# A Fourier group folded over tokens t and 256-t, in a one-layer encoder block on one core

## The chip, the cores and the metric

The kernel runs on one core of one Trainium2 chip. The metric is the device time of one execution in microseconds. The kernel before takes 934.45 us (median of three runs, 934.38 to 934.88). TensorE is the matrix engine (PE in the profile), VectorE is DVE, ScalarE is ACT, GpSimd is POOL, and SyncE (SP) issues most of the DMAs. Every engine takes its instructions in the order in which the program lists them; an instruction that waits holds up all that stand behind it on the same engine.

## The reference

One layer with 256 tokens of width 2048: a norm, a combined projection, attention heads beside Fourier groups, an output projection, a second norm, a gated feed-forward part with a short convolution, and a last norm.

```
h = RMSNorm(x)
[q | k | v | u] = h @ w_in          # 12 query heads, 4 key and value heads, u has 512 columns
a = RMSNorm(window_attention(q, k, v))
# Fourier group: u as 4 groups g of 128 channels c, s = the token
f = real(fft2(u[s, g, c], axes=(s, c), norm='ortho'))
y = einsum('sgc,gcd->sgd', f, w_fourier)
x = x + concat[a, RMSNorm(y)] @ w_out
x = x + conv_ffn(RMSNorm(x)) ; out = RMSNorm(x)
```

The real part of the two-dimensional transform is, in the positions, a product of u with cos and one with sin, for the frequencies 0 to 128 and 1 to 127; the rest follow by symmetry. In the channels it is folded with w_fourier into one small matrix each for the cosine part and the sine part.

## The kernel before, in words

Precision comes from splitting: a float32 matrix is written as a high part (rounded to TensorE's fast type) and a low part (the rest), and a product is made of three products: high by high, high by low, low by high. ScalarE writes a high part, VectorE subtracts and writes the low part.

The weights come in *units* of 1 MB (128 partitions by 2048). Units 0 to 3 are the columns of u (they come together with the transposed tokens), 4 to 7 those of v, 8 to 23 the sixteen key and query heads (k0, q0, q1, q2, k1, ...), 24 to 39 the output projection; then the feed-forward part follows. The function `unit(i, work)` sets the order by hand: it runs what is listed *before* unit i, then the unit's matmuls, then what is listed *beside* it, then `step(i)`, which splits unit i+2 (`split_high` on ScalarE, `split_low` on VectorE, after which SP issues the load of a later unit into one of three buffers), then what is listed *behind* it. The lists are filled with `at(beside, i, f, ...)`.

A unit of v (`moving_weights`, lines 347 to 349) is 24 matmuls of 512 columns. A unit of a head (`still_weights`, line 364) takes for each of 16 blocks one matmul with the high part of the weights against 512 columns and one with the low part against 256; it begins with two high ones, so it needs the low part almost at once.

The part around the change:
- The norm's row sums come from ScalarE (`token_sums`); `token_scales` makes the scale of each token, r1, with a power on GpSimd, beside unit 4. A token's scale is one value per partition. As a row (r1b, the same 256 values on each partition) it is needed to scale the keys; `row_by_hbm` (lines 318 to 322, behind unit 4) writes it value by value to HBM from GpSimd's queue and reads it back on all partitions.
- Beside unit 5, `rows_out` (466, 467) scales u from the two PSUM banks ps_u[0] (tokens 0 to 127) and ps_u[1] (tokens 128 to 255) and writes u_hi and u_lo. `fourier_positions` (530, 531) splits the table of cos and sin of the positions, 256 columns for each token block.
- Before unit 6, `fourier_weights` (545) makes the channel matrices; `fourier_weights_out` (552) copies them from PSUM as G.
- Before unit 7, `fourier_rows` (566) makes the position transform: four groups, two token blocks, three products each, 24 matmuls of 256 columns into one bank a group (ps_f). Beside unit 7 the four results go to SBUF (575, 577).
- Before units 8 to 11, `fourier_channels` (585) makes one group each (ps_y): two plain float32 matmuls, of 129 and 127 columns. Beside it the copy (593), behind it the join of the two halves (598 to 602), beside the next unit the output (`feature_out`: square, high part, low part, 495, 296, 297).
- The heads run beside units 9 and later: query head h in unit s has its scores before unit s+2, softmax beside it, and its values some units later.

Of the kernel before, what the change touches and what calls it, by code (L numbers as in the profile page):

```python
# [21 lines left out]
NG = 4  # L22
# [8 lines left out]

U_HEAD, U_ROW = 16, 768


SHIFT = 16

# [82 lines left out]
def block_kernel(  # L119
# [19 lines left out]
    nc = tc.nc  # L139
# [75 lines left out]
    cat_pool = pa.enter_context(tc.tile_pool(name="cat", bufs=16))  # L215
# [2 lines left out]
    vec = base.tile([P, 232], F32, tag="vec", name="vec")  # L218
    chan = cat_pool.tile([P, 512], F32, tag="cat", name="chan")[:, 0 : 2 * P]
    wfs = cat_pool.tile([P, FW], F32, tag="cat", name="wfs")  # L220
    pos = cat_pool.tile([P, 2, S], F32, tag="cat", name="pos")
    Gs = [cat_pool.tile([P, FW], F32, tag="cat", name=f"G{c}") for c in range(2)]
    pos_hi = cat_pool.tile([P, 2, S], F32R, tag="cat", name="pos_hi")
    pos_lo = cat_pool.tile([P, 2, S], F32R, tag="cat", name="pos_lo")
# [62 lines left out]
    ps = bank(dn, "ps_warm")  # L287
# [27 lines left out]

    rows = ctx.enter_context(tc.tile_pool(name="rows", bufs=1, space=bass.MemoryType.DRAM))

    def row_by_hbm(r, dst, name):

        row = rows.tile([2, P], F32, tag="row" + name, name="row" + name)  # L320
        nc.gpsimd.dma_start(row.rearrange("b p -> p b"), r)
        nc.gpsimd.dma_start(dst, row.rearrange("b p -> (b p)").partition_broadcast(P))


    def blocks_out(src, t, name):
# [73 lines left out]
    for c in range(4):  # L399
        t = base.tile([P, 4, 512], F32R, tag=f"hT{c}", name=f"hT{c}")  # L400
        hT.append(t)
    ps_u = [bank(mm, f"ps_u{b}") for b in range(2)]
    for k in range(NK):
        c, q = k // 4, k % 4
        if q == 0:
            hi, lo = (t.rearrange("p (k c) -> p k c", k=4) for t in parts_of(c))
        n = 1 if c < 2 else 2
# [3 lines left out]
        if q % n == 0:  # L411
            w, h = u_part(k, 0, FW, n), hi[:, q : q + n, :]
# [3 lines left out]
        if k < 4:  # L416

            for p, w in enumerate([hi, hi, lo]):
                for b in range(2):
                    o = p % 2 * S + b * P  # L420
                    nc.tensor.matmul(
                        ps_u[b], hk(k)[:, o : o + P], w[:, q, :],
                        start=k == 0 and p == 0, stop=False,
# [9 lines left out]
    ph = pa.enter_context(tc.tile_pool(name="pa", bufs=1))  # L433
# [4 lines left out]
    r1 = base.tile([P, 2], F32, tag="rstd1", name="rstd1")  # L438
# [23 lines left out]
    def rows_out(hi, lo, ps):  # L462

        for b in range(2):
            r = r1[:, b : b + 1]
            nc.scalar.activation(hi[:, b, :], ps[b], AF.Copy, scale=r)
            nc.vector.scalar_tensor_tensor(
                lo[:, b, :], ps[b], r, f32(hi[:, b, :]), ALU.mult, ALU.subtract
            )
# [7 lines left out]
    u_hi, u_lo = row_parts("u")  # L477
    v_hi, v_lo = row_parts("v")
    r1b = ph.tile([P, S], F32, tag="r1b", name="r1b")
    for c in range(2, 4):  # L480
        at(beside, 4, token_sums, c)
    at(beside, 4, lambda: fourier_parts())
    at(beside, 4, token_scales)
    at(beside, 5, rows_out, u_hi, u_lo, ps_u)
    at(behind, 5, query_scales)

    cat = {}

# [38 lines left out]
    held = {}  # L527

    def fourier_positions():
        nc.scalar.activation(pos_hi, pos, AF.Copy)  # L530
        nc.vector.tensor_tensor(pos_lo, pos, f32(pos_hi), ALU.subtract)

    def fourier_parts():
        for src, (hi, lo) in (
# [18 lines left out]

    H = S // 2
    us = []

    def fourier_rows():
        for g in range(NG):  # L560
            ps = held["f", g] = bank(dn, f"ps_f{g}")
            for b in range(2):
                for n, (u, w) in enumerate(
                    [(u_hi, pos_hi), (u_hi, pos_lo), (u_lo, pos_hi)]
                ):
                    nc.tensor.matmul(
                        ps[:, 0:S], u[:, b, g * P : (g + 1) * P], w[:, b, :],
                        start=b == 0 and n == 0, stop=b == 1 and n == 2,
                    )

    def fourier_rows_out():
        for g in range(NG):
            t = ph.tile([P, 512], F32, tag="sc", name=f"uf{g}", bufs=4)[:, 0:S]
            if g % 2:
                nc.scalar.activation(t, held.pop(("f", g))[:, 0:S], AF.Copy)
            else:
                nc.vector.tensor_copy(t, held.pop(("f", g))[:, 0:S])
            us.append(t)

    sq_f = ph.tile([P, S], F32, tag="sqf", name="sq_f")  # L580

    def fourier_channels(g):
        ps = held["y", g] = bank(dn, f"ps_y{g}")
        for part, o, n in ((0, 0, H + 1), (1, H + 1, H - 1)):
            nc.tensor.matmul(
# [3 lines left out]


    def fourier_channels_copy(g):
        h = held["h", g] = ph.tile([P, S], F32, tag="tmp", name=f"yh{g}", bufs=2)
        nc.scalar.activation(h, held.pop(("y", g))[:, 0:S], AF.Copy)

    def fourier_channels_join(g):
        h = held.pop(("h", g))
        y = held["y", g] = ph.tile([P, S], F32, tag="add", name=f"y{g}", bufs=2)
        nc.vector.tensor_tensor(y[:, 1:H], h[:, 1:H], h[:, H + 1 : S], ALU.add)
        nc.vector.tensor_tensor(
            y[:, H + 1 : S], h[:, H - 1 : 0 : -1], h[:, S - 1 : H : -1], ALU.subtract  # L600
        )
        nc.vector.tensor_copy(y[:, 0 : H + 1 : H], h[:, 0 : H + 1 : H])

# [13 lines left out]
    at(beside, 5, fourier_positions)  # L617
    at(before, 6, fourier_weights)
    at(beside, 6, fourier_weights_out)
    at(behind, 4, row_by_hbm, r1, r1b, "1")  # L620
    at(before, 7, fourier_rows)
    at(beside, 7, fourier_rows_out)
    at(beside, 8, lambda: rows_out(v_hi, v_lo, ps_v))
    at(behind, 8, distances)

    def fourier_channels_steps():
        for g in range(NG):
            i = 8 + g
# [255 lines left out]
    for n, (c, kq) in enumerate(OUT_ORDER):  # L884
        i = N_OUT + n
# [35 lines left out]
    r2b = fp.tile([P, S], F32, tag="r2b", name="r2b", bufs=1)  # L921
# [195 lines left out]
    held = {(c, p): bank(dn, f"ps_{p}_{c}") for c in range(2) for p in ("P1", "N5")}  # L1117
# [108 lines left out]
    def last_out_post(c, part, ps):  # L1226

        i = n_front + 2
        out_add(c, part, ps)
        flip_x_out(c)  # L1230
        for o, n in ((0, 512), (512, 1536)):
            split_low(i - 1, o, n)
        out_sums(c)
        split_high(i)
        split_low(i, 0, 1024)
        tot2 = base.tile([P, 2], F32, tag="tot2", name="tot2")
        nc.vector.tensor_reduce(tot2, ssq2, mybir.AxisListType.X, ALU.add)
        rstd_of(tot2, D, "2", r=r2b[:, 0:2])
        split_low(i, 1024, 1024, reload=False)
        nc.vector.transpose(r2b[:, 32:64], r2b[:, 0:32])  # L1240
        row = rows.tile([2, 4, 32], F32, tag="row2", name="row2")
        for b in range(2):
            nc.sync.dma_start(row[b], r2b[b:P:32, 32:64])
        flip_x_in(c)
        nc.sync.dma_start(r2b, row.rearrange("b q j -> (b q j)").partition_broadcast(P))
        load(i + RAW)

    OPEN = 4
# [2 lines left out]
    for q in range(OPEN):  # L1251
        kind, j = items[q]
        ps = bank(mm, f"ps_{kind}{j}")
# [4 lines left out]
        if q == 1:  # L1258
            i = up_index[3]
# [23 lines left out]
    for n, it in enumerate(items):  # L1283
# [8 lines left out]
        if it[0] in ("gate", "val"):  # L1292
            kind, j = it
            ps = bank(mm, f"ps_{kind}{j}")
# [4 lines left out]
        if it[0] == "product":  # L1299
            kind, g, c, p = it  # L1300
# [30 lines left out]
    i = up_index[n]  # L1331
# [54 lines left out]
def _layout(inp):  # L1386
# [3 lines left out]
    f = lambda a: np.ascontiguousarray(np.asarray(a), dtype=np.float32)  # L1390
    x = f(inp["x"]).reshape(2, P, D)
# [20 lines left out]
    start = {"q": 0, "k": AW}  # L1412
# [14 lines left out]
    def rows_by(tiles, cols):  # L1427
# [17 lines left out]
    )  # L1445
    t = np.arange(S)
    ang = 2.0 * np.pi * ((t[:, None] * t[None, :]) % S) / S
    c_pos = np.concatenate(
        [np.cos(ang[:, : S // 2 + 1]), np.sin(ang[:, 1 : S // 2])], axis=1
    )  # L1450
    c_pos = c_pos.reshape(2, P, S).transpose(1, 0, 2)
# [38 lines left out]
```

## Time and profile before

| | before |
|---|---|
| median of three runs | 934.45 us |
| the profiled execution's own time | 934.68 us |
| its span (first to last instruction) | 932.9 us |
| TensorE busy | 924.0 us, 99% |
| VectorE busy | 772.4 us, 83% |
| ScalarE busy | 542.3 us, 58% |
| granted TensorE clock | 0.997 |
| units 4 to 8 on TensorE | 27.3 to 59.4 us |

Busy time of a matmul is modelled and overlaps that of the next one, so the price of a matmul is read from the distance between starts, or from a piece of the chain that ended last. A row of a timeline gives start, duration, engine, line, operation, the tile written and those read, the count, and in brackets how long the engine stood idle before it and what released it. In the table of stretches a row gives the busy time of each engine, then the granted clock, the DMA engines' share and their GB/s. The table of DMA issues gives the time from issue to landing. On an engine that isn't the bound, idle time costs nothing.

### The profile page before, as it was taken

The numbers are of one execution on the slowest core, as the hardware profiler recorded it, in microseconds if no ns is written. First come the engines' busy times: TensorE is split into PE (matmuls) and PEld (weight loads), VectorE is DVE, ScalarE is ACT, GpSimd is POOL, SyncE is SP. The second block draws the span as 40 slices with busy tenths as digits, with TensorE's granted clock in tenths as the row PEclk, the third lists the DMA queues.
The fourth block names the chain that finished last, engine by engine and source line by source line (L and its number), as shares of the span: only waits on it lengthen the run. The fifth ranks groups of instructions, "written<-read, shape, count | busy, mean of one in ns | idle before, by whom it ended". The sixth has DMA issues, their size and how long they took to land.

```text
span 932.9 us, 12860 instructions
## 1 busy us (share of the span) xinstructions
PE 924.0 (99%) x4981; PEld 800.8 (86%) x4981; DVE 772.4 (83%) x988; ACT 542.3 (58%) x675; POOL 63.0 (7%) x80
## 2 busy tenths in 40 slices
PE   9999999999999999999999999999999999999996
PEld 7888998888888888888888888888888888888885
DVE  7668988787768877898878997888979789989995
ACT  7756776546455655566555665555755556655553
POOL 0101111200000000000000000000000000000002
PEclk9999999999999999999999999999999999999998
DMA  9965877657778668788798779887787968779652
GB/s 365 316 216 169 248 237 209 209 180 276 229 264 275 201 200 261 242 276 261 230 288 256 239 212 299 224 261 234 264 243 241 309 221 271 238 234 272 204 180 91
DMA packets 59309, 224.96 MB, mean 241 GB/s; under 512 B 24400, under 2 KB 29904, under 8 KB 35696
## 3 DMA queue, kind: packets, MB, share of 16 engines
q1 hardware_dynamic: 54560, 194.39, 58.3%
q0 software_dynamic: 4544, 29.49, 17.1%
q8 instruction: 39, 0.64, 0.3%
q10 hardware_dynamic: 144, 0.26, 0.1%
q14 instruction: 22, 0.18, 0.1%
HBM read 217.04 MB, written 7.08 MB: 240 GB/s over the span
## 4 chain that ended last, share of the span: by engine, by line
PE 98%; DMA 0%; ACT 0%; DVE 0%; issue 0%; POOLq 0%; POOL 0%; ACTq 0%
PE ps_val L364 25%; PE ps_gate L364 25%; PE ps_q L364 7%; PE ps_P L1161 3%; PE ps_P L1160 3%; PE ps_P L1162 3%; PE ps_N L1160 3%; PE ps_N L1161 3%; PE ps_N L1162 3%; PE ps_a L347 2%; PE ps_k L364 2%; PE ps_a L349 2%; PE ps_a L348 2%; PE ps_s L676 1%; PE ps_o L770 1%; PE ps_ff L347 1%
## 5 line engine op out<-in xcount | busy, mean ns | idle before, releaser
L203 DVE TENSOR_TENSOR lo<-raw,hi 128x2048 fp32r<-128x2048 f32 (+2 forms) x133 | 294.9, 2220 | 31.9 <-ACT hi L195 31.5
L195 ACT ACTIVATE hi<-raw 128x2048 fp32r<-128x2048 f32 (+1 forms) x131 | 246.8, 1886 | 28.2 <-PE ps_a L348 10.2
L364 PE MATMUL ps_gate<-hU,hi 128*128 128x512 f32 x688 | 236.2, 389 | 0.0
L364 PE MATMUL ps_val<-hU,hi 128*128 128x512 f32 x688 | 236.2, 389 | 0.0
L364 PE MATMUL ps_gate<-hU,lo 128*128 128x256 f32 x688 | 190.0, 276 | 0.0
L364 PE MATMUL ps_val<-hU,lo 128*128 128x256 f32 x687 | 189.7, 276 | 0.0
L364 PEld LDWEIGHTS ps_val<-hU,hi 128*128 128x128 f32 x688 | 129.2, 188 | 26.9
L364 PEld LDWEIGHTS ps_gate<-hU,hi 128*128 128x128 f32 x688 | 129.1, 188 | 26.8
L364 PEld LDWEIGHTS ps_gate<-hU,lo 128*128 128x128 f32 x688 | 129.2, 188 | 1.3
L364 PEld LDWEIGHTS ps_val<-hU,lo 128*128 128x128 f32 x687 | 129.0, 188 | 1.3
L941 ACT ACTIVATE ft_g<-ps_gate 128x256 f32<-128x256 f32 x43 | 16.5, 384 | 120.6 <-PE ps_gate L364 120.6
L941 ACT ACTIVATE ft_v<-ps_val 128x256 f32<-128x256 f32 x43 | 16.4, 383 | 86.7 <-PE ps_val L364 86.7
L364 PE MATMUL ps_q<-hT,hi 128*128 128x512 f32 x192 | 65.0, 391 | 0.0
L1160 PE MATMUL ps_P<-hi_P,op_P 128*128 128x512 f32 x144 | 56.1, 389 | 0.0
L1161 PE MATMUL ps_P<-hi_P,op_P 128*128 128x512 f32 x144 | 56.0, 389 | 0.0
L1162 PE MATMUL ps_P<-lo_P,op_P 128*128 128x512 f32 x144 | 56.0, 389 | 0.0
L364 PE MATMUL ps_q<-hT,lo 128*128 128x256 f32 x192 | 51.3, 277 | 0.0
L1058 DVE TENSOR_TENSOR lo_N<-sumw,hi_N 128x2048 fp32r<-128x2048 f32 (+1 forms) x20 | 41.5, 2076 | 9.4 <-ACT hi_N L1057 9.2
L1160 PE MATMUL ps_N<-hi_N,op_N 128*128 128x512 f32 x108 | 42.0, 389 | 0.0
L1161 PE MATMUL ps_N<-hi_N,op_N 128*128 128x512 f32 x108 | 42.0, 389 | 0.0
L1162 PE MATMUL ps_N<-lo_N,op_N 128*128 128x512 f32 x108 | 42.0, 389 | 0.0
L364 PEld LDWEIGHTS ps_q<-hT,hi 128*128 128x128 f32 x192 | 35.2, 188 | 6.6
(402 smaller groups left out, 1588.8 us busy)
## 6 DMA issues: line engine op xcount, KB each, us to landing
raw<-in_w_up SPq DMA_DIRECT2D x86, 1024.0 KB, 6.8
raw<-in_w_in SPq DMA_DIRECT2D x20, 1024.0 KB, 7.2
raw<-in_w_out SPq DMA_DIRECT2D x16, 1024.0 KB, 5.0
sumw<-in_w_down POOLq DMA_DIRECT2D x16, 1024.0 KB, 8.6
raw<-in_w_down_late SPq DMA_DIRECT2D x4, 1024.0 KB, 6.9
raw<-in_w_down_last SPq DMA_DIRECT2D x4, 768.0 KB, 4.3
turnp<-flip SPq DMA_DIRECT2D x44, 64.0 KB, 1.9
flop<-turnp SPq DMA_DIRECT2D x11, 256.0 KB, 3.2
```

Source lines behind the costliest of these rows:

```text
L195: nc.scalar.activation(halves[i][0][:, s], raws[i][:, s], AF.Copy)
L203: nc.vector.tensor_tensor(lo[:, s], raws[i][:, s], f32(hi[:, s]), ALU.subtract)
L347: nc.tensor.matmul(ps, ah, wh, start=first and q == q0, stop=False)
L348: nc.tensor.matmul(ps, al, wh, start=False, stop=False)
L349: nc.tensor.matmul(ps, ah, wl, start=False, stop=last and q == q0 + len(kk) - 1)
L364: nc.tensor.matmul(ps[:, x], (hi, lo)[i][:, k * P : (k + 1) * P], hk(k)[:, x], start=n == 0 and k == 0, stop=n == len(order) - 1 and k == ...
L676: nc.tensor.matmul(ps[:, b * S : (b + 1) * S], qT[:, qo + b * P : qo + (b + 1) * P], kT[:, ko : ko + S], start=n == 0, stop=n == 2,)
L941: nc.scalar.activation(tmp, ps[:, S : 2 * S], AF.Copy)
L1058: nc.vector.tensor_tensor(lo, src, f32(hi), ALU.subtract)
L1160: nc.tensor.matmul(ps, o[:, 0, p, :], hi[:, s], start=first and p == 0, stop=False)
L1161: nc.tensor.matmul(ps, o[:, 1, p, :], hi[:, s], start=False, stop=False)
L1162: nc.tensor.matmul(ps, o[:, 0, p, :], lo[:, s], start=False, stop=last and p == n - 1)
```

## The change

The position transform uses the symmetry of the input as well: cos takes the same value for tokens t and 256-t, sin the opposite one. So the sum u[t] + u[256-t] needs cos alone, over 128 values of t, and the difference needs sin alone.

- Token 256-t lies on another partition of another block than t. `fold_turned` (beside unit 5) scales and copies ps_u[1] to SBUF on ScalarE, and VectorE turns it twice by 32 x 32 blocks, reversing each block of 32 tokens. `fold_back` (behind unit 5) moves the four blocks of 32 partitions to their places with five DMAs on ScalarE's queue: three of 32 partitions, one of 31, one of a single partition (2 KB a partition), into the tile `back`.
- `fold` (beside unit 6, ahead of the copies of G) adds and subtracts on VectorE, u_hi is written on ScalarE; `fold_low` (behind unit 6) writes u_lo.
- The position table has 384 columns in place of 2 x 256. Frequencies are sorted, even ones first; low parts of the tables are written into columns of their own, so that a high part of u passes over high and low columns in one matmul. `fourier_rows(g)` now has four matmuls a group, of 256, 130, 320 and 192 columns, and `fourier_rows_out(g)` adds the low columns to the high ones (ScalarE copies, VectorE adds).
- The position transform moves from before unit 7 to before unit 9, its results beside units 9 and 10, the channel steps from units 8 to 11 to units 10 to 13. The copy of a channel result becomes two copies, one with its columns put back in order.
- The norm's row goes by blocks, as the second norm's did: VectorE turns it by 32 x 32 blocks, SP writes two pieces to HBM behind unit 4 and reads the row back behind unit 5. GpSimd's two DMAs are gone.

```diff
-    def row_by_hbm(r, dst, name):
-        row = rows.tile([2, P], F32, tag="row" + name, name="row" + name)
-        nc.gpsimd.dma_start(row.rearrange("b p -> p b"), r)
-        nc.gpsimd.dma_start(dst, row.rearrange("b p -> (b p)").partition_broadcast(P))
+    def row_out(t, name):
+        nc.vector.transpose(t[:, 32:64], t[:, 0:32])
+        row = rows.tile([2, 4, 32], F32, tag="row" + name, name="row" + name)
+        for b in range(2):
+            nc.sync.dma_start(row[b], t[b:P:32, 32:64])
+        return row
+    def row_in(row, t):
+        nc.sync.dma_start(t, row.rearrange("b q j -> (b q j)").partition_broadcast(P))
...
+    def fold_turned():
+        t, w = (ph.tile([P, 512], F32, tag="sc", name=f"u_{n}", bufs=4) for n in ("1", "turned"))
+        nc.scalar.activation(t, ps_u[1], AF.Copy, scale=r1[:, 1:2])
+        nc.vector.transpose(w, t)
+        w = w.rearrange("p (f i) -> p f i", i=32)[:, :, ::-1]
+        nc.vector.transpose(t.rearrange("p (f i) -> p f i", i=32), w)
+        folded["turned"] = t
+    def fold_back():
+        t = folded.pop("turned")
+        back = folded["back"] = ph.tile([P, 512], F32, tag="sc", name="u_back", bufs=4)
+        for q in range(3, -1, -1):
+            n, p = 32 - (q == 0), 97 - 32 * q
+            nc.scalar.dma_start(back[p : p + n], t[32 * q : 32 * q + n])
+        nc.scalar.dma_start(back[0:1], t[31:32])
+    def fold():
+        back = folded.pop("back")
+        for q, op in enumerate((ALU.add, ALU.subtract)):
+            t = ph.tile([P, 512], F32, tag="sc", name=f"u_fold{q}", bufs=4)
+            nc.vector.scalar_tensor_tensor(t, ps_u[0], r1[:, 0:1], back, ALU.mult, op)
+            nc.scalar.activation(u_hi[:, q, :], t, AF.Copy)
+            folded[q] = t
+    def fold_low():
+        for q in range(2):
+            nc.vector.tensor_tensor(u_lo[:, q, :], folded.pop(q), f32(u_hi[:, q, :]), ALU.subtract)
...
+    nc.gpsimd.memset(r1b[:, 0:32], 1.0)
+    def token_row_out():
+        nc.vector.tensor_copy(r1b[:, 0:2], r1)
+        held["row"] = row_out(r1b, "1")
+    def token_row_in():
+        row_in(held.pop("row"), r1b)
...
-    at(beside, 5, rows_out, u_hi, u_lo, ps_u)
+    at(beside, 5, fold_turned)
+    at(behind, 4, token_row_out)
+    at(behind, 5, token_row_in)
     at(behind, 5, query_scales)
+    at(behind, 5, fold_back)
+    at(beside, 6, fold)
+    at(behind, 6, fold_low)
...
     def fourier_positions():
-        nc.scalar.activation(pos_hi, pos, AF.Copy)
-        nc.vector.tensor_tensor(pos_lo, pos, f32(pos_hi), ALU.subtract)
+        odd = H // 2
+        n = odd + H
+        tt = nc.vector.tensor_tensor
+        cos, last, od, sin = pos[:, 0:H], pos[:, H : H + 1], pos[:, 2 * H - odd : 2 * H], pos[:, 2 * H :]
+        nc.scalar.activation(pos_s[:, H:], cos, AF.Copy)
+        nc.scalar.activation(pos_s[:, H - 1 : H], last, AF.Copy)
+        tt(pos_s[:, 0 : H - 1], cos[:, 1:], f32(pos_s[:, H + 1 :]), ALU.subtract)
+        nc.scalar.activation(pos_d[:, 0:n], pos[:, 2 * H - odd :], AF.Copy)
+        nc.scalar.activation(pos_d[:, n + H - 1 :], sin[:, 0:1], AF.Copy)
+        tt(pos_d[:, n : n + H - 1], sin[:, 1:], f32(pos_d[:, odd + 1 : n]), ALU.subtract)
...
+    def fourier_rows(g):
+        ps = held["f", g] = bank(dn, f"ps_f{g}")
+        c, o = slice(g * P, (g + 1) * P), 2 * H - H // 2
+        for n, (t, q, x, w, s) in enumerate([
+            (u_hi, 0, pos_s, 2 * H, 0),
+            (u_lo, 0, pos_s[:, H - 2 :], H + 2, H - 2),
+            (u_hi, 1, pos_d, H // 2 + 2 * H, o),
+            (u_lo, 1, pos_d, H // 2 + H, o),
+        ]):
+            nc.tensor.matmul(
+                ps[:, s : s + w], t[:, q, c], x[:, 0:w], start=n == 0, stop=n == 3,
+                skip_group_check=True,
+            )
+    def fourier_rows_out(g):
+        ps = held.pop(("f", g))
+        low = ph.tile([P, S], F32, tag="tmp", name=f"uf_low{g}", bufs=2)
+        t = us[g] = ph.tile([P, 512], F32, tag="sc", name=f"uf{g}", bufs=4)
+        nc.scalar.activation(
+            low.rearrange("p (a k) -> p a k", a=2),
+            ps.rearrange("p (a k) -> p a k", a=4)[:, 0:4:3, :], AF.Copy,
+        )
+        nc.scalar.activation(t[:, 0:1], ps[:, H : H + 1], AF.Copy)
+        nc.vector.tensor_tensor(t[:, 1:S], ps[:, H + 1 : 3 * H], low[:, 0 : S - 1], ALU.add)
...
-        h = held["h", g] = ph.tile([P, S], F32, tag="tmp", name=f"yh{g}", bufs=2)
-        nc.scalar.activation(h, held.pop(("y", g))[:, 0:S], AF.Copy)
+        h, ps = ph.tile([P, S], F32, tag="tmp", name=f"yh{g}", bufs=2), held.pop(("y", g))
+        held["h", g] = h
+        nc.scalar.activation(
+            h[:, 0:H].rearrange("p (m e) -> p e m", e=2),
+            ps[:, 0:H].rearrange("p (e m) -> p e m", e=2), AF.Copy,
+        )
+        nc.scalar.activation(h[:, H:S], ps[:, H:S], AF.Copy)
...
-    at(behind, 4, row_by_hbm, r1, r1b, "1")
-    at(before, 7, fourier_rows)
-    at(beside, 7, fourier_rows_out)
     at(beside, 8, lambda: rows_out(v_hi, v_lo, ps_v))
+    for g in range(NG):
+        at(before, 9, fourier_rows, g)
+        at(beside, 9 + g // 2, fourier_rows_out, g)
...
-            i = 8 + g
+            i = 10 + g
             at(before, i, fourier_channels, g)
```

More of the change, by code (lines that the diff above doesn't have):

```diff
@@ L32 @@
 U_HEAD, U_ROW = 16, 768
+H = S // 2
+N_POS = 3 * H
 SHIFT = 16
@@ L220, in block_kernel @@
     wfs = cat_pool.tile([P, FW], F32, tag="cat", name="wfs")
-    pos = cat_pool.tile([P, 2, S], F32, tag="cat", name="pos")
+    pos = cat_pool.tile([P, 512], F32, tag="cat", name="pos")[:, 0:N_POS]
     Gs = [cat_pool.tile([P, FW], F32, tag="cat", name=f"G{c}") for c in range(2)]
-    pos_hi = cat_pool.tile([P, 2, S], F32R, tag="cat", name="pos_hi")
-    pos_lo = cat_pool.tile([P, 2, S], F32R, tag="cat", name="pos_lo")
+    pos_s = cat_pool.tile([P, 512], F32R, tag="cat", name="pos_s")[:, 0 : 2 * H]
+    pos_d = cat_pool.tile([P, 512], F32R, tag="cat", name="pos_d")[:, 0 : H // 2 + 2 * H]
     chan_parts = cat_pool.tile([P, 2, 2 * P], F32R, tag="cat", name="chan_parts")
@@ L477, in block_kernel @@
     u_hi, u_lo = row_parts("u")
+    folded = {}
+    def fold_turned():
[22 more added lines that the diff above has]
+            nc.vector.tensor_tensor(u_lo[:, q, :], folded.pop(q), f32(u_hi[:, q, :]), ALU.subtract)
     v_hi, v_lo = row_parts("v")
     r1b = ph.tile([P, S], F32, tag="r1b", name="r1b")
+    nc.gpsimd.memset(r1b[:, 0:32], 1.0)
[4 more added lines that the diff above has]
+        row_in(held.pop("row"), r1b)
     for c in range(2, 4):
@@ L552, in fourier_weights_out @@
             nc.scalar.activation(Gs[part], held.pop(("g", part)), AF.Copy)
[L556 to L578, printed above, removed]
+    us = {}
+    def fourier_rows(g):
[21 more added lines that the diff above has]
+        nc.vector.tensor_tensor(t[:, 1:S], ps[:, H + 1 : 3 * H], low[:, 0 : S - 1], ALU.add)
     sq_f = ph.tile([P, S], F32, tag="sqf", name="sq_f")
@@ L1239, in last_out_post @@
         split_low(i, 1024, 1024, reload=False)
[L1240 to L1243, printed above, removed]
+        row = row_out(r2b, "2")
         flip_x_in(c)
-        nc.sync.dma_start(r2b, row.rearrange("b q j -> (b q j)").partition_broadcast(P))
+        row_in(row, r2b)
         load(i + RAW)
@@ L1447, in _layout @@
     ang = 2.0 * np.pi * ((t[:, None] * t[None, :]) % S) / S
[L1448 to L1451, printed above, removed]
+    near, k = ang[:H], np.r_[np.arange(0, H, 2), np.arange(1, H, 2), H]
+    even = (k % 2 == 0) * 1.0
+    c_pos = np.zeros((P, N_POS))
+    c_pos[:, 0 : H + 1] = np.cos(near[:, k])
+    c_pos[0, 0 : H + 1] = even
+    c_pos[0, 2 * H - H // 2 : 2 * H] = 1.0
+    c_pos[1:, 2 * H + 1 :] = np.sin(near[1:, 1:H])
     k = np.arange(P)
```

## The prediction

> **What bounds the kernel now.** I read the page first (engine shares, the chain that ended last), then TensorE's waits, then the timelines of TensorE, ScalarE and VectorE from 36 us on, where the changed code runs, then the DMA views.
>
> ```profile
> PE 924.0 (99%) x4981; PEld 800.8 (86%) x4981; DVE 772.4 (83%) x988; ACT 542.3 (58%) x675; POOL 63.0 (7%) x80
> PE 98%; DMA 0%; ACT 0%; DVE 0%; issue 0%; POOLq 0%; POOL 0%; ACTq 0%
> PE ps_warm L289 <- POOL ones L281: 1.0, 1, 1.0
> PE ps_u L421 <- ACT hT L296: 0.2, 1, 0.2
> ```
>
> TensorE is the bound: its two waits lie at the very start. So a matmul taken out is worth its whole issue time, and a wait that TensorE has not had so far is lost time that nothing later gives back.
>
> **The matmuls of the position transform.** Durations of matmuls overlap, so I go by distances between starts and by pieces of the chain.
>
> ```profile
> 45.21 2.88 PE ps_f L566 x24
> 53.52 0.44 PE ps_y L585 x4
> 175.01 0.44 PE ps_t L725 x4
> 45.05 0.28 PE L566 MATMUL ps_f<-pos_hi,u_hi 128*128 128x256 f32 x1
> 47.92 0.39 PE L347 MATMUL ps_v<-hi,hT 128*128 128x512 f32 x1
> 51.78 0.39 PE L349 MATMUL ps_v<-lo,hT 128*128 128x512 f32 x1
> ```
>
> The 24 removed matmuls of 256 columns cost 2.88 us, 0.12 each; one of 512 columns costs 0.227 (17 of them lie between the last two starts, 3.86 us). So a column beyond 256 costs 0.42 ns. Each group now has four: 256 columns 0.12, 320 columns 0.12 + 64 x 0.42 ns = 0.147, and two narrower ones, 130 and 192 columns, of a kind that this kernel never runs under 256. Lower end: by the column, 0.067 and 0.093, 0.427 a group, 1.71 in all, a gain of 1.17. Upper end: the channel matmuls (ps_y) of 127 and 129 columns show two records of 0.11 each, so 0.22 for some 128 plain float32 columns; at that price 0.22 and 0.33, 0.817 a group, 3.27 in all, a loss of 0.39. [...] I take 0.11 and 0.115: 0.492 a group, 1.97 in all, **a gain of 0.91 us**. The channel matmuls are the same, two units later; the weight products (ps_g) stay.
>
> **The fold, and what queues behind it.** This is the expensive part.
>
> ```profile
> 38.36 1.27 ACT L466 ACTIVATE u_hi<-ps_u,rstd 128x512 fp32r<-128x512 f32 x2 [3.26 <-POOL rstd L307]
> 39.51 0.63 ACT L530 ACTIVATE pos_hi<-pos 128x512 fp32r<-128x512 f32 x1
> 40.03 1.91 ACT L195 ACTIVATE hi<-raw 128x2048 fp32r<-128x2048 f32 x1
> 41.84 1.07 ACT L552 ACTIVATE G<-ps_g 128x512 f32<-128x512 f32 x2
> 42.79 1.93 ACT L195 ACTIVATE hi<-raw 128x2048 fp32r<-128x2048 f32 x1
> 39.75 0.74 DVE L467 SCALAR_TENSOR_TENSOR u_lo<-ps_u,rstd,u_hi 128x512 fp32r<-128x512 f32 x1
> 41.98 2.29 DVE L203 TENSOR_TENSOR lo<-raw,hi 128x2048 fp32r<-128x2048 f32 x1 [0.90 <-ACT hi L195]
> 44.46 0.17 DVE L460 RECIPROCAL rq_inv<-rq_pos 128x2 f32<-128x2 f32 x1
> 44.75 2.29 DVE L203 TENSOR_TENSOR lo<-raw,hi 128x2048 fp32r<-128x2048 f32 x1
> 81.89 0.71 DVE L328 STREAM_TRANSPOSE flip<-sc 128x512 f32<-128x512 f32 x1
> 928.32 0.37 ACTq L1223 DMA_DIRECT2D out_y<-z_P  x1
> ```
>
> Before, ScalarE and VectorE made u's parts at 38.36 to 40.5 without waiting for any transfer, then unit 7's parts (lo done 44.27) and unit 8's (lo done 47.04). Now:
> - ScalarE copies ps_u[1] at 38.36, 0.64 (half of 1.27), done 39.0. VectorE turns it twice, 0.71 each, the second waiting for the first: 39.05 to 40.5. The copy and small transpose for the norm's row lie before that, in VectorE's idle time up to 39.08.
> - ScalarE's position copies are narrower (four, some 0.7 in all) and replace 0.63 + 0.63; unit 7's high part starts near 39.6 and ends 41.5, its low part 43.8, with the scales 44.3 as before.
> - ScalarE's queue issues five DMAs, 0.37 each. They need the second transpose (40.5) and come in program order behind unit 7's high part. If the queue runs ahead of the running activation, they go at 40.55, 40.9, 41.3, 41.66 (the 31 rows) and 42.0; if it doesn't, 0.95 later. I take the first.
> - Landing:
>
> ```profile
> turnp<-flip SPq DMA_DIRECT2D x44, 64.0 KB, 1.9
> DMA to landing us min/median/max: 1.7/2.0/5.4
> q1 hardware_dynamic: 54560, 194.39, 58.3%
> q10 hardware_dynamic: 144, 0.26, 0.1%
> 41.00:42.00 1.00, 1.00 (x6) 0.82 (x5) 0.10 (x2) 1.00 (x2) 0.00 (x0) 1.00 0.96 402
> 43.00:44.00 1.00, 1.00 (x6) 0.84 (x5) 1.00 (x1) 1.00 (x1) 0.00 (x0) 1.00 0.00 0
> ```
>
> The second row is that of the tile turnp (44 DMAs). A 32-row piece of 64 KB is like it: 1.9. The 31 rows, 62 KB, have no row like them. ScalarE's only DMA before (q10) is 128 rows in 144 packets, which is 16 engines with eight rows and one closing packet each: equal shares. 31 is prime and has equal shares on one engine only. Lower end: spread all the same, 1.9. Upper end: one engine, at the rate of 194.39 MB / (0.583 x 16 x 932.9 us) = 22.3 GB/s, 2.8 us on top: 4.7; with the slowest turnp, 8.2. The shares of q10 are the nearest row, so I take 4.7, and 0.6 for the weight loads on the same engines (share 0.96 until 42, and unit 10's load again from about 44): **landing 5.3, at 47.0**. [...] No trace here shows an uneven DMA yet.
> - Behind that wait stand, on VectorE, the two fold instructions and unit 8's low part; on ScalarE, the two high parts of u, the two G copies and unit 8's high part. From the landing: fold 0.67 + 0.75, the second u_hi 0.63, G 1.07, hi 1.92, lo 2.29, less some 0.15 for overlaps: 7.2. Unit 8's low part is done at 54.2, where it was done at 47.04.
> - TensorE gets there sooner: without ps_f in front of it unit 7 starts at 45.05, takes 24 x 0.227 = 5.45 and ends at 50.5. Unit 8 starts with two high tiles (0.45) and then needs the low part: at 50.95. Before, that need came at 54.4 against 47.04, 7 us of slack; now TensorE waits 54.2 - 50.95 = **3.25 us**. Ends: landing hidden up to 44.4 (VectorE is busy till then) gives 0.65; landing at 50 gives 6.3.
>
> **Moved and cheap parts.** The norm's row: SP issues two small DMAs behind unit 9's load and the broadcast behind unit 10's (the two loads below); SP has nothing else between them, and r1b's first reader comes at 60.34. Nothing is late by it. POOL loses two issues, and its queue has nothing else there. The change takes away the old row's writes:
>
> ```profile
> 37.78 0.33 SPq L179 DMA_DIRECT2D raw<-in_w_in  x1
> 44.30 0.33 SPq L179 DMA_DIRECT2D raw<-in_w_in  x1
> 60.34 0.42 DVE L657 TENSOR_TENSOR add_k<-add_k,r1b 128x256 f32<-128x256 f32 x1
> row<-rstd POOLq DMA_DIRECT2D x1, 1.0 KB, 11.1
> 50.30 0.59 POOL L322 DMA_DIRECT2D r1b<-row  x1 [10.73 <-DMA row<-rstd]
> ```
>
> Beside them the DMA engines moved nothing at 43 to 44 us although loads were in flight. TensorE waited for none of these loads, so I count this at nothing. The low parts of u (two of 0.69) now stand before unit 9's low part: 56.7 or so against a need near 61.
>
> The join, output and copies of the four channel groups come two units later, when attention heads run. The tightest place is the fourth head's scores:
>
> ```profile
> 95.73 0.72 PE ps_s L676 x6
> 93.36 0.42 DVE L297 SCALAR_TENSOR_TENSOR qT<-add_q,qT 128x256 fp32r<-128x256 f32 x1 [0.48 <-ACT qT L296]
> 79.17 0.28 DVE L599 TENSOR_TENSOR y<-yh 128x127 f32<-128x127 f32 x1
> 83.49 0.48 DVE L297 SCALAR_TENSOR_TENSOR cat<-y,vec,cat 128x256 fp32r<-128x256 f32 x1
> ```
>
> Its qT was ready 1.95 us ahead. VectorE gets a join (0.28 + 0.2 and the small copy, starts 0.2 apart: 0.47) in unit 12 and join and output (0.87) in unit 13, 1.34 more; TensorE gets 0.88 more there (two ps_y). VectorE also comes some 0.5 later out of unit 8 and the four row outputs. About 1 us is left, so nothing, but this cover is thin.
>
> **Sum**, against the profiled execution (934.68 us, span 932.9): -0.91 + 3.25 = +2.3, 937.0. The median of the runs shown is 0.23 lower, so **936.8**.
>
> **Rivals.**
> 1. *Hidden transfer (not slower).* The 31 rows spread over 16 engines after all and land by 44.4, beneath unit 7's low part. For: turnp's 1.9. Against: the equal shares of q10. The wait is then 0.65 and the sum -0.3: 934.2. It decides from a landing before 44.7 (wait 0.91, no change); from 46.5 on it is slower by 0.2%, about what a measurement of this kernel tells from no change (1.87 us).
> 2. *Narrow matmuls at the plain float32 price.* For: ps_y's two records. Against: no record of the split type is that slow. 1.3 more: 938.1.
> 3. *A second wait at the fourth head's scores.* ScalarE's extra copies or VectorE's row outputs use up the last 1 us and 1 more: 937.8.
> 4. *TensorE loses speed in the wait.* The trace shows a slow start although the granted clock is 1.00:
>
> ```profile
> 1.00 3.36 PE L289 MATMUL ps_warm<-ones 128*128 128x128 f32 x14 [1.00 <-POOL ones L281]
> ```
>
> That is 0.24 a record against 0.11 later. If a wait near 4 us brings this back for some 3.4 us, half of that is lost on top: with 4.3 of wait, 934.45 - 0.91 + 4.3 + 1.7 = 939.5. Against it: my wait is shorter than that. [...]
>
> **How the numbers follow.** Forecast 0.42, rival 1 0.24, rival 2 0.20, rival 3 0.08, rival 4 0.06. The forecast itself spreads with the landing (46 to 48.2), 935.8 to 938.0, and some two thirds of it lie beyond 0.2%. Slower: 0.28 + 0.19 + 0.08 + 0.06 and a little of rival 1, 0.62. Faster needs the by-column price and rival 1's landing and still more, 0.04. The same: 0.34. The range goes from rival 1 (934.2) to short of rival 4 (939.2).
>
> **What would show it.** After: one wait of TensorE in unit 8 (ps_k), released by VectorE's lo, about 3 us; ps_f in 16 records, about 1.97 us; a landing of `back` over 4 us, the 31-row piece slowest; VectorE's fold waiting for that DMA; no hole in the DMA rate at 43 to 50 us. I am wrong if `back` lands before 45, if lo for unit 8 isn't behind the fold, or if TensorE waits elsewhere.

## The result and the profile after

The changed kernel takes 942.8 us (runs of 942.67 and 942.85) against 934.39 before (median of six): ratio 1.0089, 95% interval 1.0069 to 1.0109. It is slower, by more than the range of the prediction allowed (934.2 to 939.2). Some executions, four of the six of the changed kernel among them, take 15 to 20 us longer; the times and ratios here leave them out. The traces compared are those of executions of 934.68 and 942.85 us, 8.17 apart.

The page of the changed kernel first: engine shares, the granted clock in 40 slices, and the shares of the chain that ended last.

```profile
PE 926.2 (98%) x4973; PEld 800.9 (85%) x4973; DVE 776.2 (82%) x997; ACT 544.0 (58%) x689; POOL 62.6 (7%) x79
...
PEclk9979999999999999999999999999999999999998
...
PE 93%; DMA 4%; ACT 1%; DVE 1%; SPq 0%; POOL 0%; issue 0%; ACTq 0%; POOLq 0%
```

TensorE has eight matmuls fewer and yet is busy 2.2 us longer. The chain, 98% TensorE before, now has 4% DMA and some ScalarE and VectorE. And the third slice (47 to 71 us) has a granted clock of 0.7 to 0.8. The waits of TensorE say where:

```profile
PE ps_k L372 <- ACT hi L197: 4.9, 1, 4.9
PE ps_k L372 <- DVE lo L205: 1.1, 1, 1.1
PE ps_warm L291 <- POOL ones L283: 1.0, 1, 1.0
PE ps_u L429 <- ACT hT L298: 0.2, 1, 0.2
```

The two lower rows are those of before. The two upper ones are new and both lie in unit 8 (ps_k): first its high part is missing, then its low part. The chain that ended last, in order of time (start, duration, what), leads back to the fold's transfer:

```profile
42.47 1.13 ACTq L503
...
43.64 6.31 DMA u_back<-u
...
49.97 0.07 DVE u_fold L511
...
50.64 0.75 DVE u_fold L511
...
51.95 1.06 ACT G L615 x2
53.02 1.81 ACT hi L197
...
54.85 2.30 DVE lo L205
...
57.19 7.61 PE ps_k L372 x30
64.80 1.93 PE ps_f L631 x16
```

Read it downward: the last piece lands at 49.97, then come fold, the copies of G, unit 8's high part, its low part (done 57.14), and only then do 30 of unit 8's 32 matmuls run, in 7.61 us. The copies of G show how a waiting instruction holds up those behind it: the last matmul that they read ended at 39.06, and they ran at 51.95, behind the high parts of u, ahead of which ScalarE stood idle for 9.51. In the chain of the kernel before, all 32 took 5.47:

```profile
53.97 5.47 PE ps_k L364 x32
```

The position transform behind them now takes 1.93. TensorE's own timeline gives the gap of the changed kernel: the last matmul of unit 7 and the first two of unit 8.

```profile
49.59 0.39 PE L357 MATMUL ps_v<-lo,hT 128*128 128x512 f32 x1
54.87 1.22 PE L372 MATMUL ps_k<-hT,hi 128*128 128x512 f32 x2 [4.88 <-ACT hi L197]
```

Unit 8 could have begun 0.227 after 49.59, at 49.82, and have asked for its low part 0.45 later, at 50.27. It got it at 57.19.

The table of stretches (busy time of PE, PEld, DVE, ACT, POOL; granted clock; DMA share; GB/s) shows why unit 8 is slow even when it has its data:

```profile
50.00:52.00 2.00, 0.00 (x0) 0.00 (x0) 1.38 (x2) 1.22 (x3) 0.00 (x0) 0.98 0.03 12
52.00:54.00 2.00, 0.00 (x0) 0.00 (x0) 0.00 (x0) 2.00 (x4) 0.00 (x0) 0.50 0.00 0
...
58.00:60.00 2.00, 2.00 (x8) 1.71 (x7) 2.00 (x2) 1.57 (x1) 0.00 (x0) 0.50 0.81 250
...
62.00:63.00 1.00, 1.00 (x7) 0.91 (x6) 1.00 (x1) 0.00 (x0) 0.00 (x0) 0.91 0.90 336
```

The granted clock falls to 0.50 near 51.9, some 2 us into the wait, and is back only near 62.2. From 57 to 62 TensorE works at about half speed: a pair of unit 8's matmuls (512 and 256 columns) takes 0.64 us (from 58.00 to 58.64), and 0.35 once the clock is back (from 62.47 to 62.82).

The account: unit 8's low part is 57.19 - 50.27 = 6.9 us late. Of this, 0.7 is no loss against the kernel before, because in this one execution TensorE was 0.66 ahead from its first matmuls on (unit 4 begins at 26.65, before at 27.31, in the other traces of the changed beginning at 27.1 to 27.5). So the wait counts 6.3, the half clock 2.35 (the third experiment below measures it), and the position transform is 2.88 - 1.93 = 0.95 shorter: 7.7 of the 8.17 measured. The rest, some 0.5, is not explained here; 0.3 of it is added late, near 272 us.

Of the transfer itself, the view of the tile u_back has the issuing instructions (duration in ns: min/median/max, then first and last start in us), and the table of DMA issues the KB of each and the median time to landing:

```profile
L503 ACTq DMA_DIRECT2D u_back<-u x4: 623/686/1128, 40.4 to 42.5; - x4
```

```profile
u_back<-u ACTq DMA_DIRECT2D x3, 64.0 KB, 2.5
...
u_back<-u ACTq DMA_DIRECT2D x1, 62.0 KB
u_back<-u ACTq DMA_DIRECT2D x1, 2.0 KB, 6.3
```

An issue takes 0.55 (the single row) to 1.13 us of ScalarE's queue, not 0.37, so the 31 rows (62 KB) go at 42.47. The pieces of 32 rows land in 2.5. The 31 rows have no landing of their own here, and the single row, issued last, at 43.64, takes 6.3 and lands when the fold starts.

The single packets in the trace tell which of the two was last. The 31 rows go as 31 packets of 2 KB, one behind the other, from 43.76 to 48.12. The single row goes as sixteen parts of 128 bytes: fifteen move between 47.74 and 48.35, the sixteenth only at 49.17, behind the 31 rows and some packets of unit 10's load. In the table of DMA queues from 48.4 to 50 us (packets, MB, share of 16 engines) it is all that is left of ScalarE's queue (q10), the part and a closing packet:

```profile
q10 hardware_dynamic: 2, 0.00, 0.1%
```

### The profile page after: what moved, and what is told of

Same layout as the page of the kernel before. It is cut to its first block, busy times and chain, and to the rows that moved or that the text cites. A ratio compares the mean times of both kernels' runs of the same rounds, so it can differ in the third digit from the quotient of the medians.

```text
span 941.1 us, 12883 instructions
## 1 busy us (share of the span) xinstructions
PE 926.2 (98%) x4973; PEld 800.9 (85%) x4973; DVE 776.2 (82%) x997; ACT 544.0 (58%) x689; POOL 62.6 (7%) x79
## 4 chain that ended last, share of the span: by engine, by line
PE 93%; DMA 4%; ACT 1%; DVE 1%; SPq 0%; POOL 0%; issue 0%; ACTq 0%; POOLq 0%
PE ps_gate L372 25%; PE ps_val L372 25%; PE ps_q L372 7%; PE ps_P L1232 3%; PE ps_P L1233 3%; PE ps_P L1234 3%; PE ps_N L1232 3%; PE ps_N L1233 3%; PE ps_N L1234 3%; PE ps_k L372 3%; PE ps_a L357 2%; PE ps_a L355 2%; PE ps_a L356 2%; DMA chan<-in_c_chan 2%; DMA ux<-in_w_u_x 1%; PE ps_s L748 1%
```

## The experiments

My theory after this reading: the loss is one wait, made by the transfer of the fold, by what stands behind it in the queues, and by the half clock that the wait brings. Open were the transfer's slowness (31 rows on one engine, or the load of unit 10 beside it), the clock's share, and the share of the other parts (the row by blocks, the matmuls).

**31 rows as 16 + 15.** Nothing else is changed.

```diff
-            n, p = 32 - (q == 0), 97 - 32 * q
-            nc.scalar.dma_start(back[p : p + n], t[32 * q : 32 * q + n])
+            for o, n in ((0, 32),) if q else ((0, 16), (16, 15)):
+                p, r = 97 - 32 * q + o, 32 * q + o
+                nc.scalar.dma_start(back[p : p + n], t[r : r + n])
```

> The 31-row piece of fold_back goes as 16 rows and 15 rows, all else as in the changed kernel. Theory (one engine carries all 31 rows, 62 KB, and sets the landing at 49.95 us): the last piece lands near 46.5 (six issues of some 0.65 us from 40.4, the last landing some 2.5 us after its issue), VectorE's wait for the transfer falls from 6.1 to about 2.7 us, TensorE's wait in unit 8 from 6.0 to about 2.5, and with the clock staying full the time is about 936 us (937.5 if the clock still falls). Rival (the pieces land late because unit 10's load shares the engines, or because five issues on ScalarE's queue are slow): the landing stays within 1 us of 49.95 and the time within 2 us of 942.7.

Measured: 942.07 us, ratio 1.0079 (1.0065 to 1.0092), almost no better. VectorE's wait, the last issue, and the DMA issues by size:

```profile
DVE u_fold L512 <- DMA u_back<-u: 5.4, 1, 5.4
```

```profile
L505 ACTq DMA_DIRECT2D u_back<-u x1: 547/547/547, 44.6 to 44.6; - x1
```

```profile
u_back<-u ACTq DMA_DIRECT2D x1, 32.0 KB, 2.0
u_back<-u ACTq DMA_DIRECT2D x1, 30.0 KB
u_back<-u ACTq DMA_DIRECT2D x1, 2.0 KB, 4.8
```

The landing came at 49.5, 0.5 sooner. The 16 rows land in 2.0 now, but the single last row, issued at 44.6, takes 4.8 and is the last. Unit 10's load of 1 MB was issued at 43.8, just ahead of it. The queues' table has only SP's queue (q1) from 45.2 to 48.4 us, and then, from 48.4 to 48.9, the single row's sixteen parts with their closing packets on q10:

```profile
q1 hardware_dynamic: 185, 1.04, 84.2%
...
q10 hardware_dynamic: 32, 0.00, 4.4%
```

So the 31 rows aren't all: the last row moved only when the load was through.

**The fold a unit later.** The transfer stays as it is; the fold is done beside unit 7, behind unit 8's low part.

```diff
-    at(beside, 6, fold)
-    at(behind, 6, fold_low)
+    at(beside, 7, fold)
+    at(behind, 7, fold_low)
```

> The fold stands beside unit 7 and its low parts behind unit 7, so that unit 8's split is ahead of it; the transfer is as in the changed kernel. Theory (the cost is what queues behind the wait, not the transfer itself): the landing stays near 50, unit 8's low part is done near 47 as before the change, TensorE waits at most some 1.2 us, for ps_u[0]'s bank (free at 51.4, wanted at 50.2), the clock stays full, and the time is about 934.7 us. If the bank is not waited for, 933.5. Rival (the late u itself is what TensorE needs): the time stays above 940.

Measured: 936.20 us, ratio 1.0017 (1.0007 to 1.0027). 6.6 of the 8.4 us are gone with the same slow transfer. The loss is thus made for the most part by what waits behind the fold, unit 8's parts, rather than by the transfer as such. The time is 1.5 us more than expected. The trace kept, of an execution of 952.45 us, has no wait for the bank; in it TensorE waits for u's low part, before the position transform:

```profile
PE ps_f L631 <- DVE u_lo L517: 1.4, 1, 1.4
```

**TensorE kept busy in the wait.** 24 matmuls of 512 columns into a bank of their own run ahead of unit 8.

```diff
+    def keep_warm():
+        ps = bank(dn, "ps_keep")
+        for n in range(24):
+            nc.tensor.matmul(ps, hk(0)[:, 0:P], hk(0), start=True, stop=True)
+    at(before, 8, keep_warm)
```

> 24 matmuls of 512 columns into a bank that nobody reads stand before unit 8, as long as the wait (5.45 us); all else as in the changed kernel. Theory (after the wait TensorE runs at half clock until 62.1, which costs some 2.9 us of the 8.2): the granted clock stays 1.00, unit 8 starts at 55.4, its low part comes at 57.1, and the time is about 939.9 us. Rival (the clock is a record without a cost): the time stays at 942.7 or goes above it.

Measured: 940.39 us, ratio 1.0062 (1.0048 to 1.0075): added work makes the kernel 2.4 us faster than the changed one. Two stretches and the chain:

```profile
54.00:56.00 2.00, 2.00 (x10) 1.65 (x9) 0.95 (x1) 2.00 (x2) 0.00 (x0) 1.00 0.00 0
...
58.00:60.00 2.00, 2.00 (x15) 1.77 (x14) 2.00 (x2) 1.77 (x1) 0.00 (x0) 1.00 0.83 225
```

```profile
55.05 2.30 DVE lo L205
...
57.39 5.26 PE ps_k L372 x30
```

The clock stays at 1.00 (15 matmuls of unit 8 in the second stretch, 8 in the changed kernel), the low part comes when it came in the changed kernel (0.2 later), and the same 30 matmuls take 5.26 in place of 7.61. The difference of 2.35 is that of the times. So the half clock's share is about 2.4 us, and the wait itself is the rest.

**The norm's row by blocks alone.** The kernel before with the new way of writing r1b, and nothing else of the change.

```diff
...
+    at(behind, 4, token_row_out)
+    at(behind, 5, token_row_in)
...
-    at(behind, 4, row_by_hbm, r1, r1b, "1")
...
```

> The kernel before with the norm's row by blocks alone; the Fourier group as before. Theory (nobody waited for the row): no change beyond 0.1%, 934.4 us; the stretch from 43 to 50 us in which the DMA engines moved almost nothing is gone, and unit 9's load lands some 5 us after its issue in place of 10.9. Rival (the two small writes from SP hold up loads behind them): 0.3 us or more slower.

Measured: 934.42 us, ratio 0.9999 (0.999 to 1.0007). One stretch of it, and the same one of the kernel before:

```profile
46.00:47.00 1.00, 1.00 (x11) 1.00 (x10) 1.00 (x2) 0.24 (x1) 0.00 (x0) 1.00 0.98 401
```

```profile
46.00:47.00 1.00, 1.00 (x11) 1.00 (x10) 1.00 (x2) 0.32 (x1) 0.00 (x0) 1.00 0.00 0
```

Where the kernel before moves 0 GB/s, this one moves 401. The loads come sooner, but TensorE waited for none of them, so nothing is gained, as counted.

**Pieces from SP, ahead of unit 10's load.** The split of the first experiment, issued on SP's queue beside unit 5, so that the load stands behind them (and behind the load, as before, the 128 KB read of the norm's row).

```diff
-                nc.scalar.dma_start(back[p : p + n], t[r : r + n])
-        nc.scalar.dma_start(back[0:1], t[31:32])
+                nc.sync.dma_start(back[p : p + n], t[r : r + n])
+        nc.sync.dma_start(back[0:1], t[31:32])
...
+    at(beside, 5, fold_back)
...
-    at(behind, 5, fold_back)
```

> fold_back's pieces (31 rows as 16 and 15) go from SP, ahead of unit 10's load, the fold where the change has it. Theory now (the last pieces land late because they are issued with or behind unit 10's 1 MB load and come through only when it is drained near 48.5; the 31 rows are the smaller part): six issues from 40.4, all before the load, landing near 46, unit 8's low part 7.2 later at 53.2, TensorE waits some 2.5 us, full clock, 936.0 us. Rival (pieces between partitions take 6 us whatever stands beside them): landing stays near 49.5 and the time near 942.

Measured: 936.09 us, ratio 1.0021 (1.0011 to 1.0031). The fold's wait and start, and the time from issue to landing:

```profile
45.79 1.41 DVE L512 SCALAR_TENSOR_TENSOR u_fold<-ps_u,rstd,u_back 128x512 f32<-128x512 f32 x2 [1.72 <-DMA u_back<-u]
```

```profile
DMA to landing us min/median/max: 2.0/2.4/3.0
```

The landing is 4.2 us sooner than in the changed kernel, and the time 6.7 lower. TensorE's waits in unit 8 are 1.6 and 0.2. The profiled execution is the slowest of its nine (939.04; the fastest took 935.65): its clock was 0.50 at 54 to 56 us, so in that execution it fell even behind this wait.

**The same with 31 rows in one piece.**

```diff
-            for o, n in ((0, 32),) if q else ((0, 16), (16, 15)):
-                p, r = 97 - 32 * q + o, 32 * q + o
-                nc.sync.dma_start(back[p : p + n], t[r : r + n])
+            n, p = 32 - (q == 0), 97 - 32 * q
+            nc.sync.dma_start(back[p : p + n], t[32 * q : 32 * q + n])
```

> fold_back from SP ahead of unit 10's load as two runs before, but with the 31 rows in one piece. Theory that the 31 rows go through one engine row by row, some 0.1 to 0.15 us each: they land 3 to 4 us after their issue at 42.3, 1 us or a little more later than with 16 and 15 rows, and TensorE waits that much longer (937 us, more if the clock falls). Rival (31 rows are spread like 32): no difference from the run with 16 and 15 rows.

Measured: 941.65 us, ratio 1.0076 (1.0063 to 1.0089).

```profile
49.73 1.41 DVE L511 SCALAR_TENSOR_TENSOR u_fold<-ps_u,rstd,u_back 128x512 f32<-128x512 f32 x2 [5.38 <-DMA u_back<-u]
```

The one piece costs 3.9 us of landing and 5.6 us of time, far more than the size I had given it. The 31 rows move one behind the other from 43.94 to 48.57. So 31 rows alone hold the fold, with the load behind them.

**Unit 10's load behind the fold.** The 31 rows are whole again and on ScalarE's queue as in the changed kernel; unit 10's load is issued by ScalarE once the fold is done, so that no weight load runs beside the transfer. The read of the norm's row (128 KB, issued by SP at 43.55) still does.

```diff
+    def load_behind(i):
+        src, n = units[i]
+        raws[i] = wp.tile([P, 2048], F32, tag="raw", name=f"raw{i}", bufs=RAW)
+        nc.scalar.dma_start(raws[i][:, 0:n], src)
...
-            load(i + RAW)
+            if i + RAW != 10:
+                load(i + RAW)
...
     def fold():
...
+        load_behind(10)
```

> The changed kernel with unit 10's load alone moved: ScalarE's queue issues it behind the fold, so that no load runs beside the pieces; the 31 rows stay in one piece on ScalarE's queue. Theory (the load holds the last pieces): landing falls from 49.95 to about 46.5, TensorE's wait from 6.0 to about 2.7, full clock, some 936.5 us. Rival (issue on ScalarE's queue and the one engine set the landing): it stays within 1 us of 49.95 and the time within 1.5 us of 942.7.

Measured: 940.58 us, ratio 1.0067 (1.0054 to 1.0081), 4 us more than expected. The fold starts only 1.3 us sooner than in the changed kernel, and the clock is 0.50 again from about 53 to 60 us:

```profile
48.66 1.41 DVE L517 SCALAR_TENSOR_TENSOR u_fold<-ps_u,rstd,u_back 128x512 f32<-128x512 f32 x2 [4.76 <-DMA u_back<-u]
```

In the DMA queues' table ScalarE's queue (q10) holds only the fold's pieces. Its rows from 45 to 48 us, and then from 46.46 to 47.68 us:

```profile
q1 hardware_dynamic: 99, 0.09, 10.0%
q10 hardware_dynamic: 54, 0.05, 6.2%
...
q10 hardware_dynamic: 16, 0.03, 6.5%
```

6.2% of sixteen engines is about one engine (6.25%). The packets show it directly: the last row of the fence holds 15 rows of 2 KB and a closing packet, and all 31 rows go one behind the other, each beginning as the one before it ends, from 43.94 to 47.67, 17 GB/s on the mean. The 31 rows, issued at 42.65, need 6.0 us to the fold's start with no weight load beside them.

**Both taken away, on ScalarE's queue.** 16 + 15 rows, and the load behind the fold: the last edit, and with it

```diff
-            n, p = 32 - (q == 0), 97 - 32 * q
-            nc.scalar.dma_start(back[p : p + n], t[32 * q : 32 * q + n])
+            for o, n in ((0, 32),) if q else ((0, 16), (16, 15)):
+                p, r = 97 - 32 * q + o, 32 * q + o
+                nc.scalar.dma_start(back[p : p + n], t[r : r + n])
```

> Both suspects taken away on ScalarE's queue: 31 rows as 16 and 15, and unit 10's load behind the fold. Theory (the engine with 31 rows and the load are two separate holds, each of which alone keeps the landing near 49): with both gone the landing is 44.6 + 2.4 = 47.0, TensorE waits some 3.5 us, and the time is 937 us, or up to 939.5 where the clock falls in that wait. Rival (the pieces from ScalarE's queue are slow in themselves, and SP's queue was what helped): landing at 48.5 or later, 941 us.

Measured: 938.57 us, ratio 1.0044 (1.0031 to 1.0058). The fold's start, the queue from 45 to 48 us, and TensorE's waits in unit 8:

```profile
46.80 1.41 DVE L518 SCALAR_TENSOR_TENSOR u_fold<-ps_u,rstd,u_back 128x512 f32<-128x512 f32 x2 [3.00 <-DMA u_back<-u]
```

```profile
q10 hardware_dynamic: 32, 0.00, 0.7%
```

```profile
PE ps_k L378 <- DVE lo L210: 1.6, 1, 1.6
...
PE ps_k L378 <- ACT hi L202: 0.8, 1, 0.8
```

A landing at 46.8, close to the expected 47.0, in a run in which neither hold is there. Even behind these short waits the clock fell, to 0.50 from about 54.8 to 58.2 us, which is part of the 4 us that are left.

The starts of the fold side by side:

| | load of unit 10 beside or behind | load put behind the fold |
|---|---|---|
| 31 rows in one piece | 49.97 (ScalarE's queue), 49.73 (SP's, load behind) | 48.66 |
| 16 + 15 rows | 49.48 (ScalarE's queue), 45.79 (SP's, load behind) | 46.80 |

So there are two causes, each of which alone holds the landing near 49. Taking away one gave 0.5 or 1.3 us, taking away both gave 3.2. The first experiment misled because it removed only one.

**Early pieces and late fold.** The SP version with 16 + 15 rows and the fold a unit later, run in two series.

```diff
-    at(beside, 6, fold)
-    at(behind, 6, fold_low)
+    at(beside, 7, fold)
+    at(behind, 7, fold_low)
```

> As the run before, and the fold beside unit 7, its low parts behind it. Theory: nothing of the fold is in front of unit 8's split, u's low part is there before unit 9, TensorE has no wait in units 7 to 9; what is left is the 0.95 us of saved matmuls, less up to 0.5 at the fourth head's scores: 933.6 to 934.1 us. Rival (VectorE's extra work in units 9 to 13 is the next bound): a wait of over 1 us at a head's scores and 935 or more.

> The version from SP with the fold beside unit 7 once more, for its distance to the kernel before: the saved matmuls alone (0.95 us) would make 933.5 us, 0.1% below; if the earlier 0.07% was chance, 934.4.

Measured: 933.71 us, ratio 0.9995 (0.9986 to 1.0004), and the second time 933.72, ratio 0.9992 (0.9983 to 1.0). TensorE's waits:

```profile
PE ps_warm L291 <- POOL ones L283: 1.0, 1, 1.0
PE ps_u L429 <- ACT hT L298: 0.2, 1, 0.2
```

They are those of the kernel before. The medians of the kernel before beside these runs were 934.43 and 934.61, so these are 0.7 and 0.9 us lower, about the 0.95 that the matmuls give. But both intervals reach 1: it may beat the kernel before by 0.1%, which these runs can't settle.

## Why the prediction was wrong

The direction, the place and the way to the wait were right: fold, what queues behind it, unit 8's low part. Two terms were not, the landing and the clock: 936.8 was forecast, 942.8 came.

- *Matmuls of the position transform*: -0.91 forecast, -0.95 measured (16 records in 1.93). The sum held, its parts did not: no run shows the 0.11 and 0.115 put for the two narrow ones. In the changed kernel the next matmul starts 0.062 us behind one of 130 columns and 0.089 behind one of 192, near the price by the column, while the one of 320 takes 0.196 (0.147 was put) and the one of 256 takes 0.138 (0.12); medians of four each, 0.485 a group against 0.492. The plain float32 price (rival 2) did not occur.
- *What queues behind the landing*: 7.2 us forecast from landing to unit 8's low part, 7.17 measured (49.97 to 57.14). Right.
- *Landing*: this is **the first term that failed**. It was put at 47.0 and came at 49.97. Three parts add up to these 3 us. The issue: 0.37 each was assumed from another DMA of ScalarE, 0.55 to 1.13 was measured, so the 31 rows went at 42.47, not 41.66 (0.8). The piece on one engine: it was put at 4.7 in all, 2.8 of it for the rows at 22.3 GB/s; with no weight load beside it it took 6.0, 3.7 of it for the rows (1.3). The load beside it: 0.6 was allowed; the changed kernel takes 7.5 from that issue to the landing, 1.5 more than without the load (0.9). That the 31 rows go through one engine was right, as their packets show (one behind the other, from 43.76 to 48.12). Right was the split, wrong what one engine does with it. The forecast took the 31 rows for the last to land. The last was the single row behind them, which had no price: in the changed kernel by its one part behind the 31 rows (49.17), in the first experiment by all its parts behind the load (4.8 us from issue to landing, against 2.5 from its issue to the fold where the load was put off).
- *TensorE's need*: at 50.95 forecast, at 50.27 measured, 0.7 sooner. That is the head start of 0.66 that this execution had from its first matmuls on; without it the forecast is right to 0.02. So the low part is 6.9 us late instead of 3.25: 3.0 from the landing, and 0.7 that is no loss against the kernel before. The forecast named one wait, for the low part; there were two, the first for unit 8's high part, which stands behind the same fold.
- *The clock*: this is **the second term that failed**, counted at nothing in the forecast and given 0.06 as rival 4. It happened, and 2.35 us were lost by it; the rival had put it at 1.7. Its condition, a wait near 4 us, was a guess of mine, which the trace of before does not show. It was met in the changed kernel (4.9), but in the run with 16 + 15 rows and the load put off the clock fell behind waits of 0.8 and 1.6.
- *Hidden transfer* (rival 1) fell: landing 49.97. *The fourth head's scores* (rival 3) cost nothing: TensorE has no wait there in the changed kernel, nor in the version with early pieces and late fold.
- *The norm's row*: counted at nothing; measured alone, 934.42 against 934.54 beside it. Its 128 KB read also runs beside the fold's last pieces, which the forecast did not count.

With the measured terms the sum is -0.95 + 6.9 + 2.35 = 8.3, against 8.17. That it comes so close is luck: without the head start it is 7.7, and some 0.5 stays unexplained. The traces agree with 7.7: unit 9 begins at 66.74, before at 59.88, where 0.88 of channel matmuls (ps_y) had run that now come later.

Left open: why six of the 31 rows were slow (see the end), and why the same pieces land 1 us later from ScalarE's queue with the load put off (46.80) than from SP's with the load behind (45.79), though the last issue is only 0.2 later (44.3 and 44.1). For the second the packets offer a cause that no run has tested: with the load put off, the read of the norm's row (128 packets of 1 KB, 44.70 to 46.27) was issued ahead of the single row, whose sixteen parts moved among them, from 45.53 to 46.28; from SP that read was issued behind (45.41), and the parts had moved by 45.50.

## What to carry to other kernels

A transfer that is put in front of an engine's queue is to be priced with all that stands behind it: moving the reader one unit later gave back 6.6 of 8.4 us here, while a split of the transfer alone gave 0.5. Count the rows of a piece that moves partitions: with 31 rows it went through one engine, with 16 and 15 it came 3.9 us sooner, once the load was out of its way. And where TensorE is the bound, a new wait can bring the half clock on top: 2.35 us here with a wait of 4.9, and in one run it fell behind waits of 0.8 and 1.6.

## What was unexpected in the hardware

- One DMA engine moved the 31 rows of 2 KB from SBUF to SBUF at 17 GB/s on the mean (3.74 us with no weight load beside them), under the 22.3 GB/s that an engine gets on the mean of the kernel's loads. It isn't the pace of every row: 25 of them took 0.084 to 0.086 us, and six took 0.14 to 0.64, 1.75 us together. Why these six are slow, the trace doesn't show.
- A 2 KB row issued just behind a 1 MB load, from another engine's queue, took 4.8 us to land, and 6.3 where one of its sixteen parts also stood behind the 31 rows; small pieces ahead of the load took 2.0 to 3.0.
- The half clock lasted about one, two or three times 3.4 us: 10.2 in the changed kernel (51.94 to 62.18), 6.8 with 16 + 15 rows, about 3.4 with the load put off as well. In these two stretches of that last run TensorE was busy 0.43 of 2 us and then, at work again, got a clock of 0.70:

```profile
52.00:54.00 2.00, 0.43 (x2) 0.00 (x1) 2.00 (x2) 2.00 (x3) 0.00 (x0) 1.00 0.21 86
54.00:56.00 2.00, 1.97 (x8) 1.75 (x9) 2.00 (x3) 2.00 (x3) 0.00 (x0) 0.70 0.39 90
```

The idle time ahead of it had no fixed length: the clock fell 2.0 us into the wait of the changed kernel, and here at about 54.8, with TensorE at work again since 54.03, behind 3.15 us (50.88 to 54.03) in which it was busy for 0.73. That the wait of 3.25 us in my forecast would cost no clock rested on no measurement.
